# Reciprocal roots of two norms computed by five GpSimd operations each, and one block sum of token tiles 4 to 7 added on GpSimd with its sign turned

## The chip, the cores and the metric

The kernel runs on one core of one Trainium2 chip. The core has five engines that run side by side, each with a queue of its own that it works through in order: TensorE (PE; its weight loads are listed as PEld), VectorE (DVE), ScalarE (ACT), GpSimd (POOL) and SyncE (SP), whose queue here only starts DMAs. An instruction that waits for a semaphore holds back all that stand behind it on its engine. TensorE writes its products to PSUM banks, and GpSimd's operands all lie in SBUF in this kernel. The metric is the device time of one execution in microseconds (us); lower is better.

## The reference

One decoder layer over 1024 tokens of width 1024, all in float32. Two branches (a diagonal state space and a causal attention with forgetting) are gated, merged and added to the input. Then follow a cross-attention into 256 memory tokens, a feed-forward part and a last norm. What the change touches are the norms ahead of the memory queries and ahead of the feed-forward part:

```python
def rms_norm(x, gain):
    xf = x.astype(jnp.float32)
    y = xf * lax.rsqrt(jnp.mean(xf * xf, axis=-1, keepdims=True) + RMS_EPS)
    return (y * gain.astype(jnp.float32)).astype(x.dtype)
...
        h = h + (gate_a * out_a + gate_b * out_b) @ w_mix_out[l]
        h = h + memory_cross_attention(rms_norm(h, norm_mem_q[l]), rms_norm(mem, norm_mem_kv[l]),
                                       w_mem_q[l], w_mem_kv[l], w_mem_o[l])
        f_a, f_b = jnp.split(rms_norm(h, norm_ffn[l]) @ w_ffn_in[l], 2, axis=-1)
        h = h + (jax.nn.silu(f_a) * f_b) @ w_ffn_out[l]
    return rms_norm(h, norm_final)
```

## The kernel before

The tokens are cut into 8 tiles of 128, which lie in SBUF as `h` (128 tokens by 1024 channels; `h_6993` to `h_7000` in the orders below are tiles 0 to 7). Each float32 product is made as three products of a high and a low part: ScalarE copies the high part (`whi`, `u2h`, `S3h`), VectorE subtracts it from the source for the low part (`wlo`, `u2l`, `S3l`), both in `split` (L211 to L213), and TensorE multiplies (L196).

A norm of a tile goes in these steps. ScalarE squares the two halves of `h` and sums them into `ss` (`rstd`, L215; the squares themselves go to `junk`). The root is formed by `rsqrt` (L221): VectorE adds the halves and epsilon (`ms`, L227), GpSimd raises to the power -0.5 (`r`, L231), and VectorE refines once by Newton's rule in three operations on a 128x1 column (`rt`, `rt`, `r`, L237 to L239). VectorE scales the tile by the root and the gain (`xs`, L255, 128x1024). TensorE turns `xs` in eight 128x128 transposes into two PSUM banks (L261), and ScalarE and VectorE take them out.

There are two such stages of eight tiles.

- The memory-query norm. The last two products of the merged branches (n = 3 and n = 4 in a loop of seven) finish the tiles: VectorE adds a bank to `h` (L694), and `scaled(t)` follows. The transposes of tiles 0 to 3 stand in TensorE's queue between the groups of the product n = 7. They go into the banks `mm` (three of them) and `misc` (one): tile 1's second half goes to `misc`, which VectorE has to have emptied by the addition of tile 3 (`h_6996<-misc`), and tile 2's halves go to `mm` banks that tile 0's `u2l` subtractions free. The transposes of tiles 4 to 7 stand later, between the blocks of the query product, and use `misc` and `pv`.
- The feed-forward norm. `mem_out(t)` multiplies and VectorE adds (L893), then `norm_blocks(t)` (L941) does the norm and cuts the turned tile into blocks. The feed-forward products follow Strassen's scheme with seven products of block sums. Tiles 0 to 3 give the blocks A11 and A12, tiles 4 to 7 give A21 and A22, from which sums S1, S2, S3 and S4 are formed on VectorE (L958 to L961), tile 4 with tile 0 and so on. S2, S3 and S1 are split at once (`put`). The negated sum S4, formed in `a12` at L961, and A22 are stored to DRAM (`r_d`, L965 and L966) and fetched and split later by `norm_rest` (L978), shortly before the products that read them. The loads of weights for these products (`w_d`) stand in the same SP queue as these stores.

Between the two stages lies the cross-attention, whose softmax uses GpSimd for a product (`pe<-pe,sm`, L858).

The order of the instructions on each engine is set when the kernel is built: a scheduler takes them by their dependencies, the order in which they were written and its own estimate of times. So an edit in one place can move instructions of all engines around it. In the stage at the very start, `InOrder` pins the order instead, and the last stage uses it for VectorE; neither is touched.

Of the kernel before, what the change touches and what calls it, by code (L numbers as in the profile page):

```python
# [9 lines left out]
F32 = mybir.dt.float32  # L10
# [4 lines left out]
ALU = mybir.AluOpType  # L15
# [4 lines left out]
P = 128  # L20
# [9 lines left out]
EPS = 1e-6  # L30
# [36 lines left out]
def f32(ap):  # L67
    return ap.bitcast(F32)
# [53 lines left out]
class Shared:  # L122
# [5 lines left out]
    def tmp(self, name, dt=F32):  # L128
        return self.pool.tile([P, D], dt, tag="tmp", bufs=5, name=name)
# [15 lines left out]
class Block:  # L145
# [69 lines left out]
    def rstd(self, src):  # L215
        ss = self.small.tile([P, 2], F32, name="ss")
        for i in range(2):
            self.A.activation(self.junk, src[:, 512 * i:512 * i + 512], AF.Square, scale=1.0 / 32, accum_out=ss[:, i:i + 1])
        return self.rsqrt(ss, parts=2)

    def rsqrt(self, ms, pool=True, parts=1, now=True):  # L221

# [377 lines left out]
def stage_tail(B, big, s2, sh, x, glu, aT, gate_d, kv_d, sums_d, w_fox_o, w_mix_out, g_mq, w_mem_q, w_mem_o, g_ffn,  # L600
               w_ffn_in, w_ffn_out, g_fin, out):
    nc, V, A, G, T, S, small, ident = B.nc, B.V, B.A, B.G, B.T, B.S, B.small, B.ident
# [321 lines left out]
    def blocks(name, mk):  # L924
        if name not in comb:
            comb[name] = [[mk(F32R, f"{name}{s}").rearrange("p (k c) -> p k c", k=2) for _ in range(2)] for s in "hl"]
        return comb[name]

    def put(name, mk, i, src, neg=False):

        hi_, lo_ = blocks(name, mk)
        for kk in range(2):
            sv = src[:, kk * 256:(kk + 1) * 256].rearrange("p (k c) -> p k c", k=2)
            hi, lo = [a[kk][:, :, i * P:(i + 1) * P] for a in (hi_, lo_)]
            if neg:
                A.activation(hi, sv, AF.Copy, scale=-1.0)
                V.scalar_tensor_tensor(out=lo, in0=sv, scalar=-1.0, in1=f32(hi), op0=ALU.mult, op1=ALU.subtract)
            else:
                B.split(hi, lo, sv)

    def norm_blocks(t):  # L941
        i = t % 4
        xs = s2.tile([P, D], F32, tag="xs", bufs=1, name="xs")
        B.norm_scale(xs, H[t], B.rstd(H[t]), gf)
        S.dma_start(h_d[t], H[t])
        ps = [B.turn(xs, b, ("misc", "pv")[b]) for b in range(2)]
        if t < 4:
            for b in range(2):
                xf = sh.half("xf")
                A.copy(xf, ps[b])  # L950
                S.dma_start(x_d[i][:, 512 * b:512 * b + 512], xf)
                put(("A11", "A12")[b], slot, i, xf)
            return
        xa, sx, s3 = tmp("xa"), tmp("sx"), sh.half("s3")
        S.dma_start(xa, x_d[i])
        a11, a12, s1n, a22 = xa[:, :512], xa[:, 512:], sx[:, :512], sx[:, 512:]
        A.copy(a22, ps[1])
        V.tensor_sub(s3, a11, ps[0])  # L958
        V.tensor_sub(s1n, ps[0], a22)
        V.tensor_sub(a11, s1n, a11)  # L960
        V.scalar_tensor_tensor(out=a12, in0=a11, scalar=-1.0, in1=a12, op0=ALU.mult, op1=ALU.subtract)  # L961
        put("S2", slot, i, a11)
        put("S3", bslot, i, s3)
        put("S1", bslot, i, s1n, neg=True)
        S.dma_start(r_d[i][:, :512], a12)  # L965
        S.dma_start(r_d[i][:, 512:], a22)  # L966

    def norm_rest(i):
        y = tmp("xr")
        S.dma_start(y, r_d[i])  # L970
        put("S4", bslot, i, y[:, :512])
        put("A22", bslot, i, y[:, 512:])

    raws, wts, ev = {}, {}, {}
# [145 lines left out]
    for t in range(4):  # L1120
        mem_out(t)
        if t:
            norm_blocks(t - 1)
        for f in late[4 * t:4 * t + 4 if t < 3 else None]:
            f()
    norm_blocks(3)
    w_first(0)
    w_first(1)
    for t in range(4, 8):
        mem_out(t)  # L1130
        if t > 4:
            norm_blocks(t - 1)
# [7 lines left out]
    for i in range(4):  # L1140
        norm_rest(i)
# [86 lines left out]
    for m, (n, p) in enumerate(seq):  # L1228
# [6 lines left out]
        if n < 3 and p in (2, 4, 6, 8):  # L1235
            t = 4 * (n - 1) + p // 2 - 1
# [12 lines left out]
    V = B.V = InOrder(B.tc, V)  # L1249
    for i in range(4):  # L1250
# [4 lines left out]
        r = refine() if i else None  # L1255
# [770 lines left out]
```

## Time and profile before

| what | us |
|---|---|
| median of three runs | 1494.33 |
| lowest and highest of the three | 1489.39, 1501.41 |
| the profiled execution, as a whole | 1493.62 |
| its span, from the first to the last instruction | 1491.9 |
| first and last of the eight memory-query scalings (L255) | 722.1, 758.3 |
| first and last of the eight feed-forward scalings (L255) | 825.9, 891.0 |

Times of single instructions below count from the start of the span. In the profile, "L255" is line 255 of the kernel before, and a name such as `xs<-h,r,gbc` tells what an instruction writes and reads. A row of TensorE's busy time is to be read against the length of the stretch: what is missing is time in which it stood still.

### The profile page before, as it was taken

Reading aid. Unit: us, or ns where it says so; the run is one execution under the profiler, and the core shown is the slowest. Engines: PE = TensorE matmul, PEld = TensorE weight load, DVE = VectorE, ACT = ScalarE, POOL = GpSimd, SP = SyncE. Lnnn points to the kernel's source line nnn. Section 1 sums busy time; section 2 is a strip of 40 time slices with the busy share of each in tenths; the row PEclk is TensorE's granted clock in tenths of the full one; section 3 lists DMA queues with packets and bytes.
Section 4 is the critical chain, followed back from the end, with each engine's and each line's share of the span. In section 5 each row is a group of like instructions: output and inputs, shape, how many; then the busy total and the mean of one; then the engine's idle time right before and its main releaser. Section 6 shows DMA issues by size and latency. Waiting matters only on the chain.

```text
span 1491.9 us, 20559 instructions
## 1 busy us (share of the span) xinstructions
PE 1454.1 (97%) x7271; PEld 1253.5 (84%) x7271; DVE 1032.5 (69%) x1851; ACT 679.7 (46%) x1210; POOL 271.6 (18%) x359
## 2 busy tenths in 40 slices
PE   8999999999999899999999999999999999999997
PEld 7889888988777678888788778888888888888886
DVE  7678544555778766789756788777777776576555
ACT  6424333423667664344445654333333333354443
POOL 1046675200211123210102200000000000101001
PEclk9999999999999999999999999999999999999999
DMA  9575668642122467778531366555555554897653
GB/s 299 132 153 119 194 179 155 186 133 34 37 44 52 129 189 220 254 226 316 172 105 57 141 241 236 171 165 162 163 163 171 168 170 152 302 392 260 200 169 113
DMA packets 203049, 258.19 MB, mean 173 GB/s; under 512 B 36329, under 2 KB 127369, under 8 KB 202434
## 3 DMA queue, kind: packets, MB, share of 16 engines
q1 hardware_dynamic: 195746, 240.10, 53.6%
q10 hardware_dynamic: 7200, 16.78, 3.0%
q8 instruction: 57, 0.93, 0.3%
q14 instruction: 46, 0.38, 0.1%
HBM read 175.56 MB, written 83.20 MB: 173 GB/s over the span
## 4 chain that ended last, share of the span: by engine, by line
PE 73%; DVE 10%; DMA 7%; ACT 4%; issue 3%; POOL 1%; SPq 1%; POOLq 0%; ACTq 0%; DVEq 0%
PE mm L196 34%; PE pv L196 16%; PE sc L196 14%; PE mm L142 4%; DMA raw<-in_w_in_dram 2%; PE misc L196 2%; DVE wlo L213 1%; DMA sums_d<-wk 1%; DMA raw<-in_w_mem_kv_dram 1%; ACT whi L212 1%; DMA h<-in_x_dram 1%; ACT pf L1834 1%; POOL r L231 1%; DVE xs L255 1%; PE sc L142 0%
## 5 line engine op out<-in xcount | busy, mean ns | idle before, releaser
L213 DVE TENSOR_TENSOR wlo<-raw,whi 128x1024 fp32r<-128x1024 f32 (+2 forms) x119 | 127.2, 1072 | 83.3 <-ACT whi L212 80.9
L212 ACT CAST whi<-raw 128x1024 fp32r<-128x1024 f32 (+2 forms) x119 | 107.4, 903 | 120.6 <-DVE raw L1015 29.0
L213 DVE TENSOR_TENSOR ol<-or,oh 128x1024 fp32r<-128x1024 f32 x73 | 92.0, 1267 | 61.7 <-ACT oh L212 60.7
L212 ACT CAST oh<-or 128x1024 fp32r<-128x1024 f32 x73 | 76.4, 1048 | 94.1 <-PE pv L196 30.3
L196 PE MATMUL mm<-uh,whi 128*128 128x512 f32 x280 | 108.7, 388 | 0.1
L196 PE MATMUL mm<-uh,wlo 128*128 128x512 f32 x280 | 107.0, 383 | 0.2 <-DVE wlo L213 0.2
L196 PE MATMUL mm<-ul,whi 128*128 128x512 f32 x280 | 107.1, 383 | 0.0
L1076 POOL TENSOR_TENSOR g<-a,c 128x512 f32<-128x512 f32 x22 | 35.3, 1605 | 363.6 <-ACT a L1075 328.4
L231 POOL TENSOR_TENSOR r<-ms,mhalf 128x1 f32<-128x1 f32 (+1 forms) x30 | 20.6, 687 | 321.1 <-DVE ms L227 253.5
L1837 POOL TENSOR_TENSOR pl<-pf,ph 128x512 fp32r<-128x512 f32 (+1 forms) x32 | 37.4, 1170 | 227.5 <-DVE ph L1836 195.3
L1834 ACT ACTIVATE pf<-sc 128x512 f32<-128x512 f32 (+1 forms) x96 | 46.6, 491 | 33.8 <-DVE sc L1830 19.2
L196 PEld LDWEIGHTS mm<-uh,wlo 128*128 128x128 f32 x280 | 53.4, 191 | 8.3 <-DVE wlo L213 0.9
L196 PEld LDWEIGHTS mm<-uh,whi 128*128 128x128 f32 x280 | 53.8, 192 | 7.1 <-DVE mc L1802 0.4
L196 PEld LDWEIGHTS mm<-ul,whi 128*128 128x128 f32 x280 | 53.6, 191 | 6.1
L196 PE MATMUL pv<-S3h,we 128*128 128x512 f32 x176 | 56.4, 380 | 0.2 <-ACT S3h L212 0.2
L1840 DVE TENSOR_TENSOR pl<-pf,ph 128x512 fp32r<-128x512 f32 (+2 forms) x64 | 35.7, 560 | 12.2 <-ACT ph L1839 11.6
L1300 POOL TENSOR_TENSOR sg<-sg,ga 128x512 f32<-128x512 f32 x16 | 26.6, 1682 | 74.9 <-DMA ga<-gate_d 30.5
L196 PE MATMUL mm<-oh 128*128 128x512 f32 x106 | 40.2, 379 | 0.0
L196 PE MATMUL mm<-ol,oh 128*128 128x512 f32 x106 | 40.2, 379 | 0.0
L196 PE MATMUL mm<-oh,ol 128*128 128x512 f32 x106 | 40.2, 379 | 0.0
L196 PE MATMUL sc<-uh,whi 128*128 128x512 f32 x104 | 39.8, 383 | 0.0
L196 PE MATMUL sc<-ul,whi 128*128 128x512 f32 x104 | 39.6, 381 | 0.0
(717 smaller groups left out, 4626.2 us busy)
## 6 DMA issues: line engine op xcount, KB each, us to landing
or<-c_d SPq DMA_DIRECT2D x77, 256.0 KB
wo<-in_w_ffn_out_dram SPq DMA_DIRECT2D x22, 512.0 KB
c_d<-g SPq DMA_DIRECT2D x44, 256.0 KB
t_d<-wo SPq DMA_DIRECT2D x44, 256.0 KB
or<-t_d SPq DMA_DIRECT2D x44, 256.0 KB
raw<-in_w_ffn_in_dram SPq DMA_DIRECT2D x20, 512.0 KB
rawb<-in_w_ffn_in_dram SPq DMA_DIRECT2D x20, 512.0 KB
raw<-in_w_in_dram SPq DMA_DIRECT2D x18, 512.0 KB
```

Of the source, the lines that this page charges most:

```text
L142: return lambda *a, **k: self.tc.keep_in_program_order(op(*a, **k))
L196: self.T.matmul(woven(ps, a).rearrange(order), l, halves(r, a).rearrange(order), start=start, stop=stop, **kw)
L212: self.copied = self.A.copy(hi, src)
L213: self.lowered = (self.G if pool_lo else self.V).tensor_sub(lo, src, f32(hi))
L231: self.G.tensor_tensor(out=r, in0=v, in1=self.mhalf[:, 0:n], op=ALU.pow)
L255: self.V.scalar_tensor_tensor(out=xs, in0=src, scalar=r, in1=gb, op0=ALU.mult, op1=ALU.mult)
L1076: G.tensor_mul(g[:, 512:], a1, c1)
L1300: self.B.G.tensor_mul(self.out[j][:, cs], self.out[j][:, cs], ga)
L1834: self.exp = A.activation(halves(pf[:, off:], 64), woven(ps[:, off:], 64), AF.Exp)
L1837: G.tensor_sub(pl[:, off:], pf[:, off:], f32(ph[:, off:]))
L1840: V.tensor_sub(pl[:, off:], pf[:, off:], f32(ph[:, off:]))
```

## The change

There are three edits.

- `rstd` calls the new `rsqrt_pool` in place of `rsqrt`. All five operations of the root are now GpSimd instructions on a 128x1 column: the sum with epsilon (`msp`), the power (`r0p`), two tensor-scalar operations on `rtp`, and a multiplication into `r0p`. The Newton step is written as r (1.5 - 0.5 v r r), as before. This holds for the 16 roots of the two stages; the roots of the first stage and of the last norm still use `rsqrt`.
- In `norm_blocks`, for tiles 4 to 7, `a12` becomes `a12 + a11` on GpSimd in place of `-a11 - a12` on VectorE.
- `norm_rest` turns the sign of S4 when it splits it: ScalarE scales by -1 and VectorE computes the low part as -source - high.

```diff
@@ -216,7 +216,18 @@
         ss = self.small.tile([P, 2], F32, name="ss")
         for i in range(2):
             self.A.activation(self.junk, src[:, 512 * i:512 * i + 512], AF.Square, scale=1.0 / 32, accum_out=ss[:, i:i + 1])
-        return self.rsqrt(ss, parts=2)
+        return self.rsqrt_pool(ss)
+
+    def rsqrt_pool(self, ss):
+
+        G = self.G
+        v, r, t = [self.small.tile([P, 1], F32, name=s) for s in ("msp", "r0p", "rtp")]
+        G.tensor_scalar(out=v, in0=ss[:, 0:1], scalar1=ss[:, 1:2], scalar2=EPS, op0=ALU.add, op1=ALU.add)
+        G.tensor_tensor(out=r, in0=v, in1=self.mhalf[:, 0:1], op=ALU.pow)
+        G.tensor_scalar(out=t, in0=r, scalar1=r, scalar2=v, op0=ALU.mult, op1=ALU.mult)
+        G.tensor_scalar(out=t, in0=t, scalar1=-0.5, scalar2=1.5, op0=ALU.mult, op1=ALU.add)
+        G.tensor_mul(r, r, t)
+        return r
 
     def rsqrt(self, ms, pool=True, parts=1, now=True):
 
@@ -958,7 +969,7 @@
         V.tensor_sub(s3, a11, ps[0])
         V.tensor_sub(s1n, ps[0], a22)
         V.tensor_sub(a11, s1n, a11)
-        V.scalar_tensor_tensor(out=a12, in0=a11, scalar=-1.0, in1=a12, op0=ALU.mult, op1=ALU.subtract)
+        G.tensor_add(a12, a12, a11)
         put("S2", slot, i, a11)
         put("S3", bslot, i, s3)
         put("S1", bslot, i, s1n, neg=True)
@@ -968,7 +979,7 @@
     def norm_rest(i):
         y = tmp("xr")
         S.dma_start(y, r_d[i])
-        put("S4", bslot, i, y[:, :512])
+        put("S4", bslot, i, y[:, :512], neg=True)
         put("A22", bslot, i, y[:, 512:])
```

The lines behind the first edit stand 11 further down in the new file, so L694 before is L705 after, and L255 is L266. Ahead of the first stage of roots the order is the same on every engine; within the two stages and up to the first feed-forward products it moves. Three places matter below. The rows give line, operation, what is written and read, and the shape of what is written.

VectorE in the memory-query norm, from tile 1's root to tile 2's scaling, before:

```order
L238 SCALAR_TENSOR_TENSOR rt_7331<-rt_7331,ms_7329 128x1
L239 SCALAR_TENSOR_TENSOR r_7330<-rt_7331,r_7330 128x1
L255 SCALAR_TENSOR_TENSOR xs<-h_6994,r_7330,gbc 128x1024
L227 TENSOR_SCALAR ms_7355<-ss 128x1
L213 TENSOR_TENSOR wlo<-raw,whi 128x1024
L237 TENSOR_TENSOR rt_7357<-r_7356 128x1
L694 TENSOR_TENSOR h_6996<-h_6996,misc 128x512
L238 SCALAR_TENSOR_TENSOR rt_7357<-rt_7357,ms_7355 128x1
L213 TENSOR_TENSOR wlo<-raw,whi 128x1024
L239 SCALAR_TENSOR_TENSOR r_7356<-rt_7357,r_7356 128x1
L227 TENSOR_SCALAR ms_7381<-ss 128x1
L255 SCALAR_TENSOR_TENSOR xs<-h_6995,r_7356,gbc 128x1024
```

And the same place after, from tile 1's last addition to tile 0's `u2l`:

```order
L705 TENSOR_TENSOR h_6994<-h_6994,mm 128x512
L266 SCALAR_TENSOR_TENSOR xs<-h_6994,r0p,gbc 128x1024
L705 TENSOR_TENSOR h_6995<-h_6995,mm 128x512
L213 TENSOR_TENSOR wlo<-raw,whi 128x1024
L266 SCALAR_TENSOR_TENSOR xs<-h_6995,r0p,gbc 128x1024
L705 TENSOR_TENSOR h_6996<-h_6996,misc 128x512
L213 TENSOR_TENSOR wlo<-raw,whi 128x1024
L705 TENSOR_TENSOR h_6997<-h_6997,sc 128x512
L266 SCALAR_TENSOR_TENSOR xs<-h_6996,r0p,gbc 128x1024
L281 TENSOR_TENSOR u2l_0_7017<-mm,u2h_0_7009 128x2x128
L281 TENSOR_TENSOR u2l_0_7019<-mm,u2h_0_7011 128x2x128
L705 TENSOR_TENSOR h_6998<-h_6998,sc 128x512
```

The addition out of `misc` stood ahead of tile 2's scaling and stands behind it now; tile 2's own addition, which stood ahead of tile 1's scaling, is now behind that; and the first `u2l`, which stood ahead of tile 3's scaling, is behind it.

GpSimd at the start of the feed-forward norm, with the softmax product `pe<-pe,sm` of the cross-attention among the roots of tiles 0 to 2, before:

```order
L858 TENSOR_TENSOR pe<-pe,sm 128x512 x11
L231 TENSOR_TENSOR r_8359<-ms_8358,mhalf 128x1
L231 TENSOR_TENSOR r_8483<-ms_8482,mhalf 128x1
L858 TENSOR_TENSOR pe<-pe,sm 128x512 x2
L231 TENSOR_TENSOR r_8609<-ms_8608,mhalf 128x1
```

And after:

```order
L869 TENSOR_TENSOR pe<-pe,sm 128x512 x11
L225 TENSOR_SCALAR msp<-ss 128x1
L226 TENSOR_TENSOR r0p<-msp,mhalf 128x1
L227 TENSOR_SCALAR rtp<-r0p,msp 128x1
L228 TENSOR_SCALAR rtp<-rtp 128x1
L229 TENSOR_TENSOR r0p<-r0p,rtp 128x1
L869 TENSOR_TENSOR pe<-pe,sm 128x512
L225 TENSOR_SCALAR msp<-ss 128x1
L226 TENSOR_TENSOR r0p<-msp,mhalf 128x1
```

A softmax product now stands between the roots of tile 0 and tile 1, and another between those of tile 1 and tile 2.

TensorE in the first feed-forward products, where tile 7 is transposed (`xs`; `wh`, `wl` are the first block of weights, `w1h`, `w1l` the second, `whi` the third), before:

```order
L196 MATMUL sc<-A12h,w1h 128x512
L196 MATMUL sc<-A12l,w1h 128x512
L196 MATMUL sc<-A12h,w1l 128x512
L261 MATMUL misc<-ident,xs 128x128 x4
L261 MATMUL pv<-ident,xs 128x128 x4
L196 MATMUL mm<-A11h,whi 128x512
L196 MATMUL mm<-A11l,whi 128x512
```

And after:

```order
L196 MATMUL sc<-A12h,wh_8757 128x512
L196 MATMUL sc<-A12l,wh_8757 128x512
L196 MATMUL sc<-A12h,wl_8758 128x512
L272 MATMUL pv<-ident,xs 128x128 x2
L272 MATMUL misc<-ident,xs 128x128 x4
L272 MATMUL pv<-ident,xs 128x128 x2
L196 MATMUL mm<-A11h,w1h 128x512
L196 MATMUL mm<-A11l,w1h 128x512
```

Tile 7's transposes stood behind the products of the second block of weights and stand ahead of them now, 24 multiplications earlier.

## The prediction

> **What bounds the kernel now.** I read the page's busy table first, then TensorE's busy time by stretches, then what TensorE waited for.
>
> ```profile
> span 1491.9 us, 20559 instructions
> ...
> PE 1454.1 (97%) x7271; PEld 1253.5 (84%) x7271; DVE 1032.5 (69%) x1851; ACT 679.7 (46%) x1210; POOL 271.6 (18%) x359
> ```
>
> TensorE is busy 97% of the span: time is lost or won only where it stands still. The roots stand in four stretches (columns: engine, busy microseconds, instructions; then clock, DMA share, GB/s):
>
> ```profile
> 720.00:740.00 20.00, 16.71 (x89) 14.14 (x89) 16.67 (x40) 11.30 (x30) 4.14 (x4) 1.00 0.27 81
> 740.00:782.00 42.00, 41.92 (x219) 36.99 (x218) 25.75 (x58) 19.33 (x49) 3.24 (x5) 1.00 0.35 113
> 820.00:860.00 40.00, 38.01 (x209) 31.05 (x208) 30.08 (x74) 24.27 (x74) 7.65 (x9) 1.00 0.35 132
> 860.00:920.00 60.00, 56.16 (x274) 47.30 (x273) 51.56 (x108) 34.00 (x85) 4.14 (x5) 1.00 0.79 276
> ```
>
> PE idle is 20.00 - 16.71 = 3.29, 0.08, 1.99 and 3.84 us. All that could be won here is their sum, 9.2 us or 0.6%. The clock reads 1.00 in each, so no throttle is in play. VectorE (DVE) is busy 75 to 86% in the last two. Of PE's waits over the whole region (total, times, longest) these two hang on the roots by name:
>
> ```profile
> PE misc L261 <- DVE xs L255: 2.8, 4, 1.5
> ...
> PE misc L867 <- DVE rt L237: 0.8, 1, 0.8
> ```
>
> **The change part by part.** *What leaves VectorE.* Each root had four short operations there:
>
> ```profile
> L227 DVE TENSOR_SCALAR ms<-ss x16: 203/208/215, 720.6 to 889.1; 128x1 f32<-128x1 f32 x16
> L237 DVE TENSOR_TENSOR rt<-r x20: 150/159/897, 721.5 to 1462.5; 128x1 f32<-128x1 f32 x20
> L238 DVE SCALAR_TENSOR_TENSOR rt<-rt,ms x20: 149/159/161, 721.7 to 1463.8; 128x1 f32<-128x1 f32 x20
> L239 DVE SCALAR_TENSOR_TENSOR r<-rt,r x20: 147/159/725, 721.9 to 1466.3; 128x1 f32<-128x1 f32 x20
> ```
>
> 16 roots x (0.208 + 3 x 0.159) = 11.0 us. The block sum is a fifth operation on tiles 4 to 7, 4 x 0.68 = 2.7 us. GpSimd (POOL) gets 16 x 4 = 64 short operations and four of 128x512. These 13.7 us lie beside TensorE's work; alone they buy nothing.
>
> *What one root costs in time.* The first root of the stage, uncontended, before:
>
> ```profile
> 719.85 0.63 ACT L218 ACTIVATE junk<-h 128x512 bf16<-128x512 f32 x1 [1.89 <-DVE h L694]
> ...
> 720.39 0.19 ACT L218 ACTIVATION_READ_ACCUMULATOR junk<-h 128x1 f32 x1
> ...
> 720.90 0.57 POOL L231 TENSOR_TENSOR r<-ms,mhalf 128x1 f32<-128x1 f32 x1 [64.61 <-DVE ms L227]
> ...
> 722.09 1.28 DVE L255 SCALAR_TENSOR_TENSOR xs<-h,r,gbc 128x1024 f32<-128x1024 f32 x1
> ```
>
> The sum of squares is read at 720.39 + 0.19 = 720.58, the scaling starts at 722.09: 1.51 us, call it c. Afterwards c is five GpSimd operations in series. The trace has the power (0.57) but no GpSimd tensor-scalar; nearest are plain short tensor-tensor operations, one feeding the next:
>
> ```profile
> 107.16 0.21 POOL L1513 TENSOR_TENSOR ES<-d,d 128x4 f32<-128x4 f32 x1
> 107.45 0.21 POOL L1511 TENSOR_TENSOR d<-EC,trg_cs 128x8 f32<-128x8 f32 x1
> ```
>
> So 0.21 each with 0.08 between. Lower bound 0.57 + 4 x 0.21 + 4 x 0.08 + 0.10 for two handovers (1.51 - 0.21 - 0.57 - 3 x 0.16 = 0.25 for five) = 1.8 us. Upper bound, if every one costs what the power does: 5 x 0.57 + 0.42 = 3.3. I take 2.0, near the plain operations, since four of the five are multiplies and adds. A gain is excluded: five in series with a 0.57 in them don't go under 1.51 at 0.21 each.
>
> *Where GpSimd and VectorE meet.* Columns of a timeline row: start, length, engine, line, operation.
>
> ```profile
> 727.64 1.22 DVE L213 TENSOR_TENSOR wlo<-raw,whi 128x1024 fp32r<-128x1024 f32 x1
> 727.80 1.46 POOL L231 TENSOR_TENSOR r<-ms,mhalf 128x1 f32<-128x1 f32 x1 [2.11 <-DVE ms L227]
> 852.33 1.04 POOL L858 TENSOR_TENSOR pe<-pe,sm 128x512 f32<-128x512 f32 x1
> 852.49 0.90 DVE L237 TENSOR_TENSOR rt<-r 128x1 f32<-128x1 f32 x1
> ```
>
> The power took 1.46 in place of 0.57 beside a VectorE subtraction with both inputs in SBUF and ended 0.40 after it; the reverse at 852.49, 0.90 for 0.16. The Trainium skill, "SBUF — State Buffer", section "SBUF: two separate sides", calls the port pair that the two share an exclusive lock, held for the whole instruction; these four rows agree. By that rule each added GpSimd operation may hold a VectorE one as well as be held; what this would make of the time is the second rival.
>
> *Memory-query norm, tiles 0 to 3.* In the new order VectorE is given the scaling of a tile directly behind that tile's last addition, and the next tile's addition behind the scaling. The roots that overlapped other work now stand in series, and the addition that frees bank misc (h_6996<-misc) is behind three of them. The rows on either side of it, before:
>
> ```profile
> 729.37 0.68 DVE L694 TENSOR_TENSOR h<-h,misc 128x512 f32<-128x512 f32 x1
> ...
> 730.11 0.66 PE L261 MATMUL misc<-ident,xs 128*128 128x128 f32 x4 [0.61 <-DVE h L694]
> ...
> 733.17 0.42 DVE L270 TENSOR_TENSOR u2l<-mm,u2h 128x256 fp32r<-128x256 f32 x1
> ...
> 736.66 0.63 PE L261 MATMUL mm<-ident,xs 128*128 128x128 f32 x4 [1.90 <-DVE u2l L270]
> ```
>
> Per tile: c + scaling 1.28 + addition 0.68 + square 0.73 (719.85 to 720.58). From 720.58 to the end of the misc addition: 3c + 3 x 1.28 + 2 x 1.41 + 0.68 = 3c + 7.3, at c = 2.0 until 733.9. TensorE's transposes into misc began at 730.11 and stand first in its queue: +3.8 us. Then square, fourth root, scaling, four u2l (0.42 each) and an addition, c + 0.73 + 1.28 + 1.68 + 0.68: 740.3 against 736.66, +3.6. The second wait runs on from the first, so the larger counts: **+3.8** (3.2 at c = 1.8; 8.8 at 3.3). Nothing covers this: PE has no other work ahead of those transposes.
>
> *Tiles 4 to 7.* Covered by the multiplications of 740 to 782 (0.08 us idle). The cover ends where tile 4's u2l must free misc for tile 5's transposes:
>
> ```profile
> 760.14 0.75 DVE L270 TENSOR_TENSOR u2l<-misc,u2h 128x256 fp32r<-128x256 f32 x2
> ...
> 762.19 0.60 PE L261 MATMUL misc<-ident,xs 128*128 128x128 f32 x4
> ```
>
> 760.89 against 762.19: 1.3 us of slack. That u2l stands behind four scalings; 4 x (2.0 - 1.51) = 2.0 us later, **+0.7** (0 to 5.9).
>
> *Feed-forward norm, tiles 0 to 3.* Tile 1's root is now behind a product pe<-pe,sm on GpSimd:
>
> ```profile
> 832.76 1.04 POOL L858 TENSOR_TENSOR pe<-pe,sm 128x512 f32<-128x512 f32 x1 [1.59 <-DVE sm L856]
> ...
> 833.85 1.28 DVE L255 SCALAR_TENSOR_TENSOR xs<-h,r,gbc 128x1024 f32<-128x1024 f32 x1
> 835.19 0.66 PE L261 MATMUL pv<-ident,xs 128*128 128x128 f32 x4 [0.25 <-DVE xs L255]
> ```
>
> The product ends at 833.80; c = 2.0 more makes 835.8 for a scaling that began at 833.85, and PE took its result after a wait of 0.25 us. Tile 0's root, 0.5 longer, costs PE 0.4; that pushes PE back, so tile 1 adds some 1.4 of its 2.0. The wait on rt, 0.8, goes. Together **+1.0** (-0.8, if both roots are covered, to +4).
>
> *Tiles 4 to 7 and the first feed-forward multiplications.*
>
> ```profile
> 885.44 0.19 ACT L218 ACTIVATION_READ_ACCUMULATOR junk<-h 128x1 f32 x1
> ...
> 889.07 0.20 DVE L227 TENSOR_SCALAR ms<-ss 128x1 f32<-128x1 f32 x1
> ...
> 892.39 0.63 PE L261 MATMUL misc<-ident,xs 128*128 128x128 f32 x4 [1.50 <-DVE xs L255]
> ```
>
> Tile 7's squares were read at 885.63, but its first short operation came at 889.07, behind block sums in VectorE's queue, and PE stood 1.50 us. A root wholly on GpSimd starts at once: 3.4 us less, 0.5 more. The new order uses this: the transposes stand 24 multiplications earlier, and laid out against the rows of before the scalings of tiles 5 to 7 come about as PE wants them. Of 3.84 us idle I take **-3.0** (bounds -3.8 and 0, if the gain is eaten by the lock).
>
> *Block sum and signs.*
>
> ```profile
> L961 DVE SCALAR_TENSOR_TENSOR xa<-xa x4: 680/682/684, 873.2 to 896.0; 128x512 f32<-128x512 f32 x4
> L1076 POOL TENSOR_TENSOR g<-a,c x22: 1492/1597/2130, 917.7 to 1287.1; 128x512 f32<-128x512 f32 x22
> 882.78 0.75 DVE L213 TENSOR_TENSOR S2l<-xa,S2h 128x256 fp32r<-128x256 f32 x2
> ...
> 883.46 0.75 DVE L937 SCALAR_TENSOR_TENSOR S1l<-sx,S1h 128x256 fp32r<-128x256 f32 x2
> ```
>
> 0.68 on VectorE becomes 1.04 (the product above) to 1.60 on GpSimd: 0.4 to 0.9 longer per tile, on data that goes to DRAM and back before S4 is needed. Queued behind that store on SP are weight loads; but tile 7's sum is formed some 3 us earlier than before, so the store isn't late. The S4 split changes its form only, 0.75 a pair in either form. **0**; with that cover gone, at most 4 x 0.9 = 3.6.
>
> **The sum.** 3.8 + 0.7 + 1.0 - 3.0 = +2.5 us on the profiled execution (span 1491.9, 1493.6 with what lies around it): 1496.1. The median of the runs, 1494.3, is 0.7 above it: 1496.8, say 1497. What a measurement can tell from no change is 1%, 15 us.
>
> **The rivals.** *Slower by over 1%: dear GpSimd operations.* If the tensor-scalars, which take their factors from memory, cost the power's 0.57 or more, c is 3.3. The terms then move by 4 us per us of c (tiles 0 to 3), 4 (tiles 4 to 7), 2 (feed-forward tiles 0 and 1) and 1 (tile 7): 2.5 + 11 x 1.3 = +16.8, 1511. It decides from c = 2.0 + 12.4/11 = 3.1. For it: rows of 1.46 in place of 0.57; against: in the first stage VectorE mostly idles while a root runs, and four of the five are plain. 0.10.
>
> *The lock eats the gain.* Five operations of 0.21 per root can hold VectorE 8 x 1.05 = 8.4 us in the feed-forward stage, as much as the 8 x 0.685 + 2.7 = 8.2 that it sheds. Then the -3.0 goes and the time is +5.5, 1500. For it the row at 852.49; against: in those four rows VectorE reads SBUF alone, and many operations here have one input in PSUM. It is what the skill's rule would make of it. 0.14.
>
> *Relief wins.* If the additions in the first stage wait less (TensorE later than its old time anyway, squares earlier), the +3.8 falls to about 1 and the sum to -0.3 to -4: 1490 to 1494. For it: 13.7 us off an engine that ends most waits; against: the order of rows. 0.18.
>
> **How the numbers follow.** Forecast (1494 to 1500) 0.58, relief 0.18, lock 0.14, dear operations 0.10. The range 1490 to 1504 takes in the first three and leaves out the last and some tails. Faster by over 1% would need more than the 9.2 us that there are: 0.02, for the spread of the runs. Slower 0.10, within 1% 0.88.
>
> **What would show it.** The length of the five rows on GpSimd gives c: right near 2.0, wrong from 3. The transposes into misc near 730 should wait 4 to 5 us on an addition, with 7 us idle in that stretch; if under 4, the series of roots is wrong. From 860 to 920 the idle time should fall to about 1 us; if it stays, the lock or the order took it. If PE waits on S4 or on a weight load, the block sum is not free.

## The result and the profile after

The changed kernel takes 1509.05 us (median of six runs, 1507.56 to 1512.21), the kernel before 1495.46 us (median of six, 1489.39 to 1501.41). The ratio is 1.0094, with a 95% interval of 1.0076 to 1.0113: slower by 14.1 us by the means, 11.4 to 16.9. The forecast was 1497, with a range of 1490 to 1504.

The page of the changed kernel, its span and the busy time of each engine:

```profile
span 1505.8 us, 20576 instructions
...
PE 1454.6 (97%) x7271; PEld 1252.4 (83%) x7271; DVE 1024.0 (68%) x1783; ACT 679.1 (45%) x1210; POOL 295.3 (20%) x427
```

VectorE is busy 8.5 us less and GpSimd 23.7 us more, as the change says. TensorE has the same instructions and the same busy time to 0.5 us; the span is 13.9 us longer, so all but 0.5 us of that is TensorE standing. The stretches with the roots show where (length, then busy microseconds and instructions of PE, PEld, DVE, ACT and POOL; clock; DMA share; GB/s; the last two rows are explained below):

```profile
720.00:740.00 20.00, 15.04 (x71) 12.67 (x70) 11.16 (x13) 9.01 (x24) 6.51 (x20) 0.91 0.32 106
740.00:790.00 50.00, 47.39 (x248) 41.19 (x247) 28.82 (x56) 22.18 (x55) 9.90 (x21) 1.00 0.30 97
820.00:860.00 40.00, 35.40 (x204) 30.17 (x203) 27.49 (x61) 24.19 (x75) 11.91 (x22) 1.00 0.29 107
860.00:935.00 75.00, 66.90 (x322) 55.50 (x321) 57.12 (x103) 40.24 (x102) 18.40 (x32) 1.00 0.67 235
732.45:735.86 3.41, 0.00 (x0) 0.00 (x0) 1.57 (x3) 1.26 (x3) 1.46 (x5) 1.00 0.51 154
735.86:739.28 3.42, 3.04 (x9) 2.60 (x10) 2.18 (x4) 2.90 (x10) 1.66 (x5) 0.50 0.22 64
```

TensorE stands 4.96, 2.61, 4.60 and 8.10 us in the first four, 20.3 in all, where before it was 3.29, 0.09, 1.99 and 3.84 in the same four, 9.2 in all. That makes 11.1 of the 13.9 us; between 790 and 820 it stands 1.0 us less (1.13 before, 0.12 after). Some 2 us more were lost ahead of the first stage, where no instruction moved: the first of its roots starts at 722.67, against 720.61 before. In the first 50 us the two traces differ by 2.5 us of standing (4.26 and 6.80), and the traces of the kernels below have anything from 4.3 to 6.7 there, so it counts as spread.

What TensorE waited for between 700 and 960 us (total, times, longest):

```profile
PE misc L272 <- DVE h L705: 4.2, 1, 4.2
PE misc L272 <- DVE xs L266: 4.2, 3, 2.1
PE misc L878 <- DVE mx L862: 2.8, 2, 1.8
PE pv L272 <- DVE xs L266: 2.4, 1, 2.4
PE misc L272 <- DVE u2l L281: 1.6, 1, 1.6
```

A row names the instruction that ended last before the wait did, which need not be the one waited for. The third is such a case: the transposes at L878 read `pe` and not `mx`, as is shown below.

The five operations of the first root, uncontended:

```profile
722.67 0.30 POOL L225 TENSOR_SCALAR msp<-ss 128x1 f32<-128x1 f32 x1 [64.31 <-ACT junk L218]
723.05 0.57 POOL L226 TENSOR_TENSOR r0p<-msp,mhalf 128x1 f32<-128x1 f32 x1
723.73 0.34 POOL L227 TENSOR_SCALAR rtp<-r0p,msp 128x1 f32<-128x1 f32 x1
724.16 0.19 POOL L228 TENSOR_SCALAR rtp<-rtp 128x1 f32<-128x1 f32 x1
724.43 0.19 POOL L229 TENSOR_TENSOR r0p<-r0p,rtp 128x1 f32<-128x1 f32 x1
724.66 1.28 DVE L266 SCALAR_TENSOR_TENSOR xs<-h,r0p,gbc 128x1024 f32<-128x1024 f32 x1 [2.85 <-POOL r0p L229]
```

From the end of ScalarE's sum of squares (722.58) to the scaling are 2.08 us: c was taken as 2.0. VectorE stood 2.85 us ahead of this scaling and 2.91 ahead of the next; before, it did the four short operations in this time, and at the second root an addition too. And the wait that was forecast for the transposes into `misc`:

```profile
734.30 1.28 DVE L266 SCALAR_TENSOR_TENSOR xs<-h,r0p,gbc 128x1024 f32<-128x1024 f32 x1 [1.84 <-POOL r0p L229]
735.51 0.68 DVE L705 TENSOR_TENSOR h<-h,misc 128x512 f32<-128x512 f32 x1
...
736.24 1.12 PE L272 MATMUL misc<-ident,xs 128*128 128x128 f32 x4 [4.20 <-DVE h L705]
```

TensorE stands 4.20 us, the addition is behind the third scaling, the scaling behind its root. But these four transposes also take 1.12 us, where they took 0.66 before. The last two rows of the stretches above tell why: from 732.45 to 735.86 TensorE did nothing, and from 735.86 to 739.28 the granted clock was 0.50. The prediction had said that no throttle is in play.

The clock of every run tells how much of this there is. One minus the granted clock, times the span, is the time that a run lost to the clock (an upper bound, since half clock costs nothing while TensorE stands). Its mean is 14.3 us for the changed kernel and 9.0 for the kernel before (29 runs). Over 106 runs of ten of the kernels here, compared within each kernel, a run that lost 1 us more to the clock took 0.78 us more. So by the means some 4 to 5 of the 14 us are half clock, an estimate, and some 9 are waits. The two profiled executions lie closer in this: 10.5 us and 9.0 are lost to the clock in them by their granted clocks (0.993 and 0.994), and in the stages of the roots the one stretch above is all the half clock that there is, 3.04 us of work at half speed, 1.5 us lost. The changed kernel's is the fastest of its six.

### The profile page after: what moved, and what is told of

Its sections match the earlier page's. It is cut to its first block, busy times and chain, and to the rows that moved or that the text cites. A ratio compares the mean times of both kernels' runs of the same rounds, so it can differ in the third digit from the quotient of the medians.

```text
span 1505.8 us, 20576 instructions
## 1 busy us (share of the span) xinstructions
PE 1454.6 (97%) x7271; PEld 1252.4 (83%) x7271; DVE 1024.0 (68%) x1783; ACT 679.1 (45%) x1210; POOL 295.3 (20%) x427
## 5 line engine op out<-in xcount | busy, mean ns | idle before, releaser
L242 POOL TENSOR_TENSOR r<-ms,mhalf 128x1 f32<-128x1 f32 (+1 forms) x14 | 9.1, 653 | 177.4 <-DVE ms L238 108.2
L196 PE MATMUL mm<-yh,whi 128*128 128x512 f32 x104 | 39.6, 381 | 0.0
```

Source lines behind the costliest of these rows:

```text
L196: self.T.matmul(woven(ps, a).rearrange(order), l, halves(r, a).rearrange(order), start=start, stop=stop, **kw)
L242: self.G.tensor_tensor(out=r, in0=v, in1=self.mhalf[:, 0:n], op=ALU.pow)
```

## The experiments

The change has three parts, and each of them also gives the scheduler another order. The first four kernels take the parts one by one, each in the order that the scheduler then makes. After that the parts are run in the order of before. All ratios are to the kernel before, "in us" is the ratio put into us; "lost" is the mean time lost to the clock (9.0 for the kernel before).

| kernel | median, us | ratio, 95% interval | in us | lost, us |
|---|---|---|---|---|
| whole change | 1509.05 | 1.0094 [1.0076, 1.0113] | +14.1 | 14.3 |
| memory-query roots alone | 1503.68 | 1.0063 [1.0038, 1.0087] | +9.4 | 12.8 |
| feed-forward roots alone | 1501.17 | 1.0047 [1.0029, 1.0065] | +7.0 | 11.2 |
| block sum and signs alone | 1499.68 | 1.0030 [1.0014, 1.0045] | +4.5 | 10.5 |
| both sets of roots | 1506.23 | 1.0082 [1.0061, 1.0103] | +12.3 | 12.0 |
| memory-query roots, additions first | 1498.98 | 1.0020 [1.0007, 1.0032] | +3.0 | 11.1 |
| memory-query roots, order of before | 1498.71 | 1.0018 [1.0002, 1.0034] | +2.7 | 9.2 |
| feed-forward roots, order of before | 1494.26 | 1.0004 [0.9989, 1.0019] | +0.6 | 8.2 |
| roots of before, order of the feed-forward roots | 1498.87 | 1.0023 [1.0005, 1.0041] | +3.4 | 9.7 |
| block sum and signs, order of before | 1496.50 | 1.0006 [0.9993, 1.0020] | +0.9 | 9.5 |
| whole change, order of before | 1500.41 | 1.0030 [1.0015, 1.0045] | +4.5 | 9.7 |
| the same, roots three operations longer | 1515.97 | 1.0132 [1.0110, 1.0153] | +19.7 | 15.1 |

### One part at a time, each in its own order

`rstd` takes `own=True` for `rsqrt_pool` and calls `rsqrt` otherwise; the block sum and the S4 sign are as before or as changed.

```diff
-        return self.rsqrt_pool(ss)
+        return self.rsqrt_pool(ss) if own else self.rsqrt(ss, parts=2)
...
-        B.norm_scale(xss[t], H[t], B.rstd(H[t]), gq[0])
+        B.norm_scale(xss[t], H[t], B.rstd(H[t], own=True), gq[0])
```

The memory-query roots:

> Only the eight roots of the memory-query norm are wholly on GpSimd; feed-forward roots, block sum and signs as before. Series of roots (the prediction's own term, 3.8 + 0.7): +4.5 us, with a wait of 4 to 5 us of the transposes into misc on an addition near 734. By the shifts between the two traces (which took in a stretch at half clock behind that wait, and 1.8 us at tiles 4 to 7): +6. If the loss is made in the feed-forward norm (VectorE held by GpSimd's additions): under +3.

+9.4 us (5.7 to 13.0): more than the series of roots (4.5), while the 6 of the shifts lies within the bounds, with the wait of 4.2 us in its place. 3.8 us of it are lost to the clock.

The feed-forward roots:

> Only the eight roots of the feed-forward norm are wholly on GpSimd, the rest as before. The prediction's terms: +1.0 - 3.0 = -2.0 us. By the shifts between the two traces, in which VectorE stands behind each root with other work queued there: +4 to +5. If the loss in this stage comes from the block sum on GpSimd, and not from the roots: -1 to +1.

+7.0 us: the roots that were to bring 2 us cost 7, without any block sum on GpSimd.

The block sum and the signs:

> Only the block sum of tiles 4 to 7 is on GpSimd with the S4 split's sign turned; all roots as before. The prediction: 0 us (at most 3.6). If GpSimd's 128x512 addition holds VectorE (after: a scaling of 2.31 us for 1.28 beside one): each of four additions takes 0.68 off VectorE and puts about 1.0 on it, +1 to +4 us. If it hides: 0.

+4.5 us (2.1 to 6.7), near the upper end (4) of what a held VectorE was to cost, and not 0.

All sixteen roots:

> All sixteen roots on GpSimd, block sum and signs as before. If the parts add up: the sum of the two runs with one half each, about +10 by the shifts between the traces, +2.5 by the prediction's terms. If the block sum is the cost: 4 us or more below the whole change (+13.6), if it is free: +13.

+12.3 us (9.1 to 15.4). By the middles the parts don't add up: 9.4 + 7.0 is 16.4, and the block sum on top of both roots adds 1.8 in place of 4.5. The bounds of these sums overlap, so that is not shown. It would fit costs that hang on an order made anew each time: in its trace the block sum alone puts at least 50 rows of TensorE in another place.

### Additions first

Of the kernel with the memory-query roots alone, the additions of tiles 1 to 3 are written and pinned ahead of the scaling of the tile before. In the trace three rows of VectorE and one of ScalarE stand in another place, none of TensorE, GpSimd or SyncE.

```diff
+            if n == 3:
+                rooted(i)
+                if i:
+                    scaled(i - 1)
+                if i == 3:
+                    scaled(3)
+            elif n == 4:
+                scaled(4 + i)
```

> As the run with the memory-query roots alone (+9.1 us), but of tiles 0 to 3 each addition of the last product is written ahead of the scaling of the tile before, so that VectorE no longer holds it behind a root; nothing else is in another order. If the loss comes from roots in series (order): the wait of 4.2 us on the addition into misc falls to about 1 us, the half clock behind it goes, and the time is +2 to +4 on before. If it comes from the length of the GpSimd operations, or from the clock for another reason: +8 or more.

+3.0 us (1.0 to 4.8), two thirds of the loss gone with these rows. The wait on the addition is gone, but another has come in its place, and the half clock did not go: 6.83 us of it begin within this wait, as within the wait of 4.2 us in the run with the memory-query roots alone. From 715 to 800 TensorE stands 5.64 us here, 7.44 there and 3.50 before, so the two traces show 1.8 of the 6.4 us between the runs; where the rest was saved stays open. TensorE and VectorE of this kernel:

```profile
734.93 1.28 DVE L809 SCALAR_TENSOR_TENSOR xs<-h,r0p,gbc 128x1024 f32<-128x1024 f32 x1 [1.76 <-POOL r0p L229]
736.13 0.75 DVE L281 TENSOR_TENSOR u2l<-mm,u2h 128x256 fp32r<-128x256 f32 x2
...
737.02 1.09 PE L272 MATMUL mm<-ident,xs 128*128 128x128 f32 x4 [4.14 <-DVE u2l L281]
```

It is the second wait of the prediction: tile 0's `u2l` stands behind four scalings. That is why the next kernel puts back the whole order.

### The order of before

Each instruction that both kernels have gets its place by a list of ranks, engine by engine, in the stage concerned; GpSimd is free. TensorE, ScalarE and SyncE then stand row for row as before, and VectorE too but for the short operations that are gone. (In the runs with the block sum, ScalarE's S4 copies have their other form.)

```diff
+RANKS = {
...
+        mine = [i for i in traced[at:] if str(i.engine).endswith("." + name)]
+        for x, y in zip(ranks, ranks[1:]):
+            B.tc.add_manual_dep(mine[y], mine[x].name, mybir.DependencyInfo(
+                mybir.DependencyClass.NoSync, mybir.DependencyReason.DATA), reason="order of another kernel")
```

> Feed-forward roots wholly on GpSimd, but every other instruction of TensorE, VectorE, ScalarE and SyncE in this stage in the order of before. If the +6.6 us of the run with these roots alone come from the new order (transposes and scalings set too early for a root of 2.05 us): 0 to +2. If from the root's length or GpSimd holding VectorE: +5 or more.

> Memory-query roots wholly on GpSimd (the run with these alone: +7.7 to +9 us), every other instruction of TensorE, VectorE, ScalarE and SyncE in this stage in the order of before, so that besides the additions the split of tile 0 (u2l) also stands ahead of the scaling of tile 3. If the order makes the loss: 0 to +2. If the longer root does: +6 or more.

> Block sum on GpSimd and turned sign alone (with its own order: +3.7 us), every other instruction of the feed-forward stage in the order of before. If the new order makes the loss: -1 to +1. If GpSimd's addition holding VectorE does (about 1 us in each of four tiles): +3 to +5.

> The whole change (+14 us in its own order), every instruction that both kernels have in the order of before, in both stages. If the order makes the loss: 0 to +3. If the operations themselves make it: +10 or more.

The feed-forward roots cost 0.6 us (-1.6 to 2.8) in place of 7.0 (4.3 to 9.7), the memory-query roots 2.7 (0.3 to 5.1) in place of 9.4 (5.7 to 13.0). For the block sum, 0.9 in place of 4.5, the intervals overlap (-1.0 to 3.0, 2.1 to 6.7), so its share is likely and not shown. The whole change costs 4.5 us (2.2 to 6.7) in place of 14.1 (11.4 to 16.9), and here the parts add up within their bounds: 2.7 + 0.6 + 0.9 = 4.2. Two thirds of the loss come from the order, a third from the operations. The traces agree: from 715 to 960 TensorE stands 10.34 us before, 20.39 in the changed kernel and 12.46 in the changed kernel with the order of before.

The reverse for the feed-forward stage, roots of before in the order made for the GpSimd roots:

> The reverse: roots as before, with power on GpSimd and four short operations on VectorE, but the other instructions of TensorE, VectorE, ScalarE and SyncE in the order that the run with the feed-forward roots on GpSimd had. If the new order itself costs: +4 to +7. If the order is good for a quick root (1.5 us) and only the longer root spoils it: -2 to +2.

+3.4 us (0.7 to 6.1), between the two expectations. The order costs something with quick roots, and by the middles more (7.0, 4.3 to 9.7) with long ones; the bounds overlap. That it is a tight order, which a longer root meets, is likely and not shown.

### A longer root

```diff
         G.tensor_mul(r, r, t)
+        G.tensor_scalar(out=t, in0=r, scalar1=r, scalar2=v, op0=ALU.mult, op1=ALU.mult)
+        G.tensor_scalar(out=t, in0=t, scalar1=-0.5, scalar2=1.5, op0=ALU.mult, op1=ALU.add)
+        G.tensor_mul(r, r, t)
```

> As the run before it, with a second Newton step in each of the sixteen roots: three GpSimd operations more, c longer by about 0.9 us. By the prediction's slope (11 us for each us of c): +10 on that run. If in the order of before other work lies behind the root: 0 to +4.

c is 3.08 us in this trace (squares read at 724.16, scaling at 727.24), 1.0 more, and the time rises by 15.6 us over the run before it (medians; 16.3 by the means). 5.4 of it are lost to the clock, which leaves 10.9. The two traces say the same: from 715 to 960 TensorE stands 23.13 us in place of 12.46, 10.7 more. That is the slope that the prediction worked out, 11 us for each us of c, though it had worked it out for the other order, so the close hit is in part luck. The order of before is no cover for a long root either.

### What a wait costs

The first of these fills the wait on `misc` in the kernel with the memory-query roots.

```diff
+            if (t, b) == (1, 0):
+                one = ident.bitcast(BF16)
+                for _ in range(36):
+                    T.matmul(ps[:, :2 * P], one[:, :P], one, start=True, stop=True)
```

> As the run with the memory-query roots alone (+9.1 us), with 36 products of the identity, whose result is overwritten, put ahead of the transposes of tile 1 so that TensorE is busy while it waits for the addition into misc. If the half clock behind that wait is made by TensorE standing idle: it is gone at this place, and the time is 2 to 4 us below that run (+5 to +7 on before) though nothing is earlier. If the clock does not hang on it: +9 or, by the added work, more.

1503.62 us, ratio 1.0066 [1.0041, 1.0090]: no faster than without the products, against the expectation. They cover the wait on `misc` (0.3 us is left of 4.2), and 1.8 us less are lost to the clock, but 2.4 us of waits on `u2l` follow, and half clock comes behind those. So waits were put where nothing else disturbs them. In the feed-forward stage of the kernel before, TensorE is busy 365.00 of the 365 us from 935 to 1300. Here it is made to wait for a chain of GpSimd operations that starts from its own product:

```diff
+        if j in (5, 9, 13, 17):
+            z, c = B.bank("misc"), B.chain[:, 0:1]
+            V.tensor_copy(c, b1[:, 0:1])
+            for _ in range(17):
+                G.tensor_scalar(out=c, in0=c, scalar1=-0.5, scalar2=1.5, op0=ALU.mult, op1=ALU.add)
+            B.late = B.tc.keep_in_program_order(T.transpose(z[:, :P], B.chain, ident)).ins
         prod(j, 7, b3, True)
```

> The kernel before, with four waits of TensorE put into the feed-forward stage, where it is otherwise busy all the time: a column copied from the bank of product 6, seventeen short GpSimd operations on it in series, and a transpose of the result ahead of product 7, for four of the 22 column blocks. Some 5 us of standing each, 20 in all. If a long wait is paid a second time in half clock (3.4 us of it behind each, 1.7 us of work lost): 5 to 8 us over the sum of the four waits in the trace, with half-clock stretches behind them. If a wait costs its length alone: the sum, within 2 us.

> The same with two GpSimd operations in place of seventeen and in twenty column blocks: some 1 us of standing each, 20 in all. By both theories the time rises by the sum of the waits alone, within 2 us, and no half clock stands behind any of them.

> As the run with twenty waits of 2.8 us, but the transpose that waits stands behind product 7 (twelve multiplications, 2.6 us) and the chain has six GpSimd operations: twenty waits of some 1.2 us. If only a wait that leaves TensorE busy for less than about 0.45 of a 3.4-us stretch is followed by half clock: no half clock in this stage, and the time rises by the sum of the waits and of the transposes, within 3 us. If every wait is paid beyond its length: 10 us or more over that sum.

The waits came out longer than planned: ahead of the first long one the copy starts 2.0 us after its product, behind other work of VectorE, and the seventeen operations take 7.03 us. TensorE's waits for the chain in the three traces, in the order of the runs (total, times, longest):

```profile
PE misc L1071 <- POOL chain L1070: 37.6, 4, 9.4
```
```profile
PE misc L1071 <- POOL chain L1070: 55.6, 20, 3.8
```
```profile
PE misc L1073 <- POOL chain L1070: 27.6, 20, 4.0
```

| waits | mean time over before, us | waits and the transposes behind them | beyond that | lost to the clock, over before |
|---|---|---|---|---|
| 4 of 9.4 us | 48.5 | 37.6 + 4 x 0.47 | 9.0 | 17.6 |
| 20 of 2.8 us | 79.0 | 55.6 + 20 x 0.33 | 16.8 | 14.8 |
| 20 of 1.4 us | 33.7 | 27.6 + 20 x 0.33 | -0.5 | -0.6 |

The times are means of five or six executions, the waits those of one; the traced executions took 6.1 and 4.4 us less and 0.5 us more than these means. So the column "beyond that" is rough. Counted in the traces, within and behind the four waits lie 11 half-clock stretches, and half of TensorE's busy time in them is 9.7 us; behind the twenty of 2.8 us lie nine, with 15.4 us, and behind the twenty of 1.4 us one, with 1.7 us.

A long wait is paid twice and a brief one once; of the waits of 2.8 us some are paid twice too, against the expectation. Here is a stretch with one of the waits of 9.4 us, then the one behind it, up to the return of the clock (the columns are now length, PE busy with its instructions, clock, DMA share, GB/s):

```profile
989.50:995.80 6.30, 6.00 (x15) 0.50 0.02 7
982.10:989.50 7.40, 0.00 (x0) 0.73 0.98 299
995.80:1002.60 6.80, 6.80 (x34) 1.00 0.00 0
```

The middle row is the wait: half clock begins within it, at 985.5, behind a stretch of 3.41 us in which TensorE did nothing. The first row is the work behind it: 15 multiplications in 6.3 us, where 34 take 6.8 at full clock. Of the waits of 2.8 us, two, each as a pair of stretches of 3.41 us that follow each other:

```profile
949.43:952.84 3.41, 1.01 (x5) 1.00 0.96 275
952.84:956.26 3.42, 3.42 (x9) 0.50 0.82 259
1014.28:1017.69 3.41, 1.73 (x9) 1.00 0.39 114
1017.70:1021.10 3.40, 2.42 (x12) 1.00 0.80 271
```

In all these traces half clock comes in stretches of 3.41 us or a multiple of it, on a fixed grid. The first wait fell within one such stretch and left TensorE busy 0.30 of it, and the next was at half clock; the second wait was cut in two by the grid, 0.51 and 0.71, and cost its length only. In this stage, of the two traces with twenty waits, every stretch with a busy share of 0.40 or less was followed by half clock and none with 0.49 or more. In the trace with four, two of 0.43 and 0.45 were not. The same in the trace of the brief waits, with one of 1.26 us:

```profile
950.31:953.72 3.41, 2.15 (x12) 1.00 0.94 265
953.73:957.14 3.41, 3.41 (x17) 1.00 0.89 296
```

The share is 0.63, and the clock stays. Eighteen of the twenty waits were of 1.2 to 1.3 us and one of 1.6, and none of these was followed by half clock; the one of 4.0 us was.

The Trainium skill, "TensorE: Matmul & The Clock Gate", section "HAM oscillation — how this bites in real kernels", gives the rule as no gaps of TensorE above some 3.4 us. That length agrees with these runs, but the rule is too mild for them: of the twenty waits of the middle run eighteen were of 2.7 us, and seven of these were followed by half clock.

## Why the prediction was wrong

**The length of a root: right.** c = 2.08 us, forecast 2.0. Operations with factors from memory take 0.30 to 0.34, with constants 0.19.

**Memory-query norm, tiles 0 to 3 (+3.8): right in place and mechanism, the size in part by luck.** The wait is on the forecast addition, 4.20 us, within the 4 to 5 named. Tile 2's second transposes start at 742.52 in place of 736.66, and with the 2.06 us that the first root is late already that is 3.8 later. But TensorE's waits in this place grew only by 2.6 us (0.61 + 0.78 + 1.90 before; 0.75 + 4.20 + 0.30 + 0.63 after), and the stretch from 720 to 740 stands 4.96 us and not the 7 named. The rest fits the half clock, 1.5 us lost, which the prediction had ruled out. Putting the additions ahead took two thirds of that stage's loss away, and what was left was the second wait that the prediction had set beside the first.

**Tiles 4 to 7 (+0.7): right in place, too small.** Tile 5's transposes waited 1.6 us on tile 4's `u2l`, inside the bounds.

**Feed-forward norm, tiles 0 to 3 (+1.0): too small, and one wait misread.** The prediction let the wait on `rt`, 0.8, go with the short operations. But the transposes that wait there read `pe`, not `rt`: the GpSimd product that makes it ended at 853.37, and `rt` 0.02 later (the prediction's rows at 852.33 and 852.49). In the changed kernel the same transposes wait 1.83 us in place of 0.84. The row names `mx`, which they don't read either; the product ended at 864.90, 0.02 ahead of it. It was late because the reciprocal `sm` stood in VectorE's queue behind tile 3's scaling, which had waited 1.18 us for its root:

```profile
862.37 1.28 DVE L266 SCALAR_TENSOR_TENSOR xs<-h,r0p,gbc 128x1024 f32<-128x1024 f32 x1 [1.18 <-POOL r0p L229]
863.58 0.16 DVE L867 RECIPROCAL sm<-sm 128x2 f32<-128x2 f32 x1
...
863.86 1.04 POOL L869 TENSOR_TENSOR pe<-pe,sm 128x512 f32<-128x512 f32 x1 [1.52 <-issue]
863.97 0.95 DVE L862 TENSOR_SCALAR mx<-mx 128x2 f32<-128x2 f32 x1
864.96 0.42 PEld L878 LDWEIGHTS misc<-ident,pe 128*128 128x128 f32 x4 [2.23 <-POOL pe L869]
864.96 0.66 PE L878 MATMUL misc<-ident,pe 128*128 128x128 f32 x4 [1.83 <-DVE mx L862]
```

With the roots of before in the order made for the GpSimd roots, TensorE waits 2.1 us at this place, and there the row names the product. So the order has a part in it.

At tile 1 the product held the scaling itself, which the prediction had not counted:

```profile
843.52 1.04 POOL L869 TENSOR_TENSOR pe<-pe,sm 128x512 f32<-128x512 f32 x1
843.61 2.04 DVE L266 SCALAR_TENSOR_TENSOR xs<-h,r0p,gbc 128x1024 f32<-128x1024 f32 x1 [1.61 <-POOL r0p L229]
...
845.70 0.44 PE L272 MATMUL pv<-ident,xs 128*128 128x128 f32 x2 [2.36 <-DVE xs L266]
```

2.04 us for 1.28: the root was late, then the scaling was held for 0.76, and TensorE waited 2.36 us where it had waited 0.25. For tile 0 it waited 1.02 in place of 0.30. The three waits together grew by 3.8 us where 1.0 was forecast.

**Feed-forward norm, tiles 4 to 7 (-3.0): the step that failed.** The prediction took the gain at tile 7 and said that the new order uses it: "laid out against the rows of before the scalings of tiles 5 to 7 come about as PE wants them". TensorE's standing from 860 to 935 did not fall by 3.0 us but rose from 3.84 to 8.10. Of this 1.83 is the wait for `pe` above, which lay ahead of 860 before; that leaves +2.4 where -3.0 was forecast. The waits in that stretch of the changed kernel:

```profile
880.96 0.63 PE L272 MATMUL misc<-ident,xs 128*128 128x128 f32 x4 [2.06 <-DVE xs L266]
...
887.43 0.63 PE L272 MATMUL misc<-ident,xs 128*128 128x128 f32 x4 [1.08 <-DVE xs L266]
...
899.36 0.63 PE L272 MATMUL misc<-ident,xs 128*128 128x128 f32 x4 [0.19 <-DVE sx L970]
...
906.33 0.48 PE L196 MATMUL pv<-S3h,we 128*128 128x512 f32 x1 [0.94 <-ACT S3h L212]
...
907.55 0.48 PE L196 MATMUL pv<-S3l,we 128*128 128x512 f32 x1 [0.74 <-DVE S3l L213]
...
909.64 0.48 PE L196 MATMUL mm<-S2l,whi 128*128 128x512 f32 x1 [0.74 <-DVE S2l L213]
```

Tile 7 did come out: its wait of 1.50 us is 0.19 now. But the new order had moved other transposes forward in TensorE's queue as well, tile 4's by 4 multiplications and tile 5's by 13 (tile 6's two groups stand 5 and 14 further back), and there the scaling is late: tile 4 waits 2.06 (before 0.66), tile 5 1.08 (0.29), and the products that read S3 and S2 wait 2.4 in all (0.43; a wait of 0.83 on S4 is gone). The prediction looked at the tile that it expected to gain and not at the tiles whose transposes the same order had set earlier. Tile 4's wait is 1.49 us with the roots of before in the order made for the GpSimd roots, and 0.77 with the GpSimd roots in the order of before: the order does more there than the root. With the order of before the feed-forward roots cost nothing that can be measured, and also bring nothing. That shows in the trace of this run at tile 7:

```profile
886.02 0.19 POOL L235 TENSOR_TENSOR r0p<-r0p,rtp 128x1 f32<-128x1 f32 x1
890.22 1.28 DVE L272 SCALAR_TENSOR_TENSOR xs<-h,r0p,gbc 128x1024 f32<-128x1024 f32 x1
...
891.64 0.63 PE L278 MATMUL misc<-ident,xs 128*128 128x128 f32 x4 [2.21 <-DVE xs L272]
```

The root is ready at 886.21, as early as was hoped, and the scaling starts 4.0 us later: it stands behind the same block sums in VectorE's queue that the short operations had stood behind. Moving the root off an in-order queue does not move what the root is for.

**Block sum and signs (0, at most 3.6).** In the order of before 0.9 us, an interval that holds 0; in its own order alone 4.5. The addition takes 1.28 to 1.40 us on GpSimd, between the 1.04 and 1.60 that were set, and VectorE is slower beside it:

```profile
884.80 1.40 POOL L972 TENSOR_TENSOR xa<-xa 128x512 f32<-128x512 f32 x1
884.97 2.31 DVE L266 SCALAR_TENSOR_TENSOR xs<-h,r0p,gbc 128x1024 f32<-128x1024 f32 x1
...
887.43 0.41 PE L272 MATMUL misc<-ident,xs 128*128 128x128 f32 x2 [1.08 <-DVE xs L266]
```

Tile 5's scaling takes 2.31 us for 1.28, 1.03 more, and TensorE waits for it. What the addition took off VectorE there (0.68) it more than gave back.

**The sum, the slope and the missing term.** The prediction put the slope at 11 us for each us of c, and the longer root shows 10.9 of waits. What it lacked was the second price: it read a clock of 1.00 in the four stretches and left the throttle out, where a long wait brings half clock by itself. The twelve waits of 3.0 us or more in all these traces, from 60 us on, each brought it, the wait of 4.20 us at once. Of the 14.1 us, the runs with the order of before leave 4.5, of which 0.7 are lost to the clock. The order makes the other 9.6, of which at most 4.6 are lost to the clock (14.3 against 9.7).

**The rivals.** Dear GpSimd operations were not it: c is far below the 3.1 from which that rival decided, yet the time came out where it had put it, within 2 us of 1511. The lock was seen on two waits of TensorE, behind tile 1's scaling and tile 5's, with 0.76 and 1.03 us, and it is part of the loss, but the same operations in the order of before cost 4.5 us in all. Relief did not come. No rival said that the new order itself, in which the scheduler sets instructions closer to a root than the root allows, is the larger part. That the scheduler sets them so close is the reading of the waits on scalings above. Whether it did so because it takes GpSimd's operations for shorter than they are was not tried.

## What to carry to other kernels

Where a scheduler sets the order, a change is two changes: the operations, and the order that it makes of all engines around them; run the new operations in the old order before you judge them, and when you lay a new order out by hand, look at every place where TensorE's instructions moved forward, not at the one that should gain. An operation moved off an in-order queue frees its own place there, but what waits for its result stands where it stood. Count a wait of TensorE that leaves it idle for the larger part of a 3.4-us stretch at its length plus some 1.7 us, one of 9.4 us at 2 to 3 us more, and one of 1.2 us at its length.

## What the runs showed of the hardware that was not expected

- Half clock follows a stretch of 3.41 us, on a fixed grid, in which TensorE was busy 0.40 or less; with 0.43 or more it did not, in the feed-forward stage. Waits of 2.7 us therefore meet it by chance, seven of eighteen here. Elsewhere in the program the point is less sharp: in the trace of before a stretch that reads 0.64 busy was followed by half clock too, and one of 0.48 in the memory-query norm of the whole change in the order of before.
- Short GpSimd operations on a 128x1 column took 0.19 us with constants or a plain product, 0.30 to 0.34 with factors from memory, 0.56 to 0.58 for the power, with 0.08 between them when one feeds the next.
- A GpSimd operation of 128x512 and a VectorE scaling of 128x1024, both on SBUF, hardly ran beside each other: the scaling took 1.28 us alone, 2.04 beside a product of 1.04 and 2.31 beside an addition of 1.40, and ended 1.08 to 1.09 us after the GpSimd operation both times. The Trainium skill, "SBUF — State Buffer", section "SBUF: two separate sides", calls this an exclusive lock for the whole instruction; these rows agree.
